# A hybrid decoder step on one core: another hand-over order for the mixer's streams

## The chip, the cores and the metric

The kernel runs on one core of a Trainium2 chip. The core's engines work side by side and meet at semaphores: TensorE (PE, with its weight loads shown as PEld), VectorE (DVE), ScalarE (ACT), GpSimd (POOL) and SyncE (SP). SP computes nothing and starts nearly all loads; POOL starts the gathered ones. The metric is the device time of one execution in microseconds (us).

## The reference

One step of a decoder layer for a prompt of 256 tokens and 64 sample tokens (8 sequences of 8), width 1024, all in float32:

```python
h = x * (1.0 + scale) + shift                     # from adaln(c): silu(c) @ w_ada + b_ada
rq, rk, rv, rg, mq, mk, mv = project(h, w_in, pos)  # one projection, split by columns
o_ret, ret_state = retention_fn(rq, rk, rv, log_g)  # 4 heads with decay
o_moba = moba_fn(mq, mk, mv)                        # 4 heads, top-3 blocks of cached K/V + own block
mixed = concat([group_norm(o_ret) * silu(rg), o_moba]) @ w_o
x = layer_norm(ALPHA * x + gate * mixed, ln_g, ln_b)
x = layer_norm(ALPHA * x + gate_f * (relu(h_f @ w_up) ** 2 @ w_down), ...)
```

The sample tokens attend to 1024 cached positions each, found through a page table; keys and values of the cache are gathered page by page. The new keys, values and retention states are outputs too.

## The kernel before

The kernel has three stretches on PE: a first one that prepares the modulation (adaLN), the modulated input `hT` and the projection `zq` (0 to 63.5 us in the trace); the mixer (63.5 to 286.9 us); and the feed-forward part (FFN) with its weights `up` and `dn` (to the end). The change concerns the mixer alone.

Nearly all the mixer's data are weights and cache pages that are used once. They come in tiles of 512 KB through one ring of ten slots (tag "wr", `WR = 10`, line 135). A load can start only when the slot's last reader is done: an ACT and a DVE instruction for projection weights, which are split into a high and a low part (`split1`, lines 177 and 179), a DVE transpose for cached keys (line 612), a matmul for adaLN weights (line 567) and cached values (line 703). SP starts its loads strictly in its own order (line 189, and line 320 for pages of V), and so does POOL (line 602 for keys, line 303 for every other page of the second half of V): an early load whose slot isn't free holds back all behind it.

The mixer's work is written as about forty generators, "streams", each of which issues a few instructions per step. The names that the text uses:

- `qk`, `mv`, `rv`, `rg`: the projections (lines 439 to 445), `lqk` ... `lrg`: their weight loads and splits
- `ga`, `gs`, `gc`: three adaLN products, eight tiles each (`Ada.step`, line 567); the sum with the bias, `gao`, `gso`, `gco`, is a DVE instruction (line 572)
- `G0`, `G1`: gathers of cached keys `kp` for two groups of four sequences; `K0`, `K1`: the transposes into the one tile `kt` (line 612), the scores `psS` (line 619) and the softmax, whose probabilities are turned by `pp` (line 677)
- `V0`, `V1`: pages of V and their products `po` (line 693 for the new tokens, line 703 for the cache); `h0` to `h3`: prompt heads; `rs`, `r0`, `r1`, `st`: the prompt's retention
- `sr`: the sample's retention: `pos` (lines 861, 864), its group norm `gs_r`, `gs_n`, `gs_y` (lines 766 to 778, on DVE, POOL and ACT), its transpose `pt7` (line 873) and the new state `pns` (line 884), for which POOL builds `vx` (line 881)
- `wl`, `w00` ... `w23`: the out-projection's weights `wo` and its products `pw`; `xl`: three loads of `x` into slots that earlier held the turned queries and keys `qkT` and the values `mvA`; `n0` to `n2`: the layer norm; `ul`, `u0`, `us`: the first FFN block

What sets the order of the mixer's work is one text, `SCHEDULE` (line 98). Each word names a stream, `*n` repeats it, and the loop at line 1188 takes one step of that stream:

```python
for step in SCHEDULE.split():
    name, _, n = step.partition("*")
    for _ in range(int(n or 1)):
        next(run[name])
```

The framework beneath keeps each engine's instructions roughly in this order, hands out slots in it, and places waits by data. So the text decides the order on all five engines at once, and with the slots also what each load has to wait for.

Of the kernel before, what the change touches and what calls it, by code (L numbers as in the profile page):

```python
# [25 lines left out]
T = SEQ + NB * TS  # L26
# [69 lines left out]


SCHEDULE = """
lqk*2 qk lmv qk*2 lmv qk mv ga G0 ga T mv ga G0 ga T ga*2 mv*2 ga T qk T*2 gs lmv*2 gs mv T mv
gs mv G0 mv ga K0 tb ga mv K0 G0 K0 mv qk mv G0 gs lqk*2 qk G0 gs K0 mv qk*3 gs K0 lrv K0 lrv  # L100
rv gs ov G0 rv gs rv gs qk*2 ok rv*2 lrv rv lrv ro K0 ro rT rv rT G0 rv ov ro rT ok gc rv K0*2
rv*2 G0*3 gc K0*2 rv lrg*2 K0*2 rg G0 rg G0 K0 gc*2 K0 G0 rg K0*2 rg G0 rg G0 K0*2 gc G1 rg K1
K0 lrg K0 G1 lrg K0 G1 rg rs G1 K1*3 gc G1 rg G1 rg*2 K1 gc*2 V0*4 rg*2 sw G1 K1 h0 sw rs gc r0
mx sw K1 sw sr h1 h0 K1 G1 h3 V0 r1 G1 V0 K1 G1 h0 h1 G1 r0 V0 G1 K1 sw*2 V0 G1 K1 G1 sr h2 K1
G1 V0 K1 V0 K1 h2 r1 G1 K1 sr K1 sr wl K1 h3 K1 st K1*2 wl w10 wl K1 h1 xl sr w00 K1 V1 w00 h2
w10 h3 w11 w20 w21 w11 wl V0 w01 w21 w20 w02 ul V1 gt w02 st w01 w03*2 w12 sc V1 w12 V1 w13 xl
n0 w13 n0 V1 ul n0 n1 n0 n1 V1*5 xl V1 n0 n1*2 u0 w23 w22 ul*2 w23 n1 u0 w22 n2*4 us u0*5 us u0
us
"""


# [1264 lines left out]
```

## Time and profile before

| | |
|---|---|
| median of 3 runs | 522.01 us (520.49 to 522.8) |
| the profiled execution | 523.97 us, span of its instructions 522.2 us |
| mean granted TensorE clock | 0.984 of full speed |
| busy PE, PEld, DVE, ACT, POOL | 490.8, 371.0, 320.2, 191.5, 119.4 us |
| moved by DMA | 122.80 MB, mean 235 GB/s |

A share of the span is an average: PE is busy for 94% of it, and the other 6% lie at a few places that the views by window and by wait show. "Granted clock" is the share of full speed (2.4 GHz) that PE got; at 0.5 it runs at its lower level, 1.2 GHz, and each matmul takes about twice as long, without any idle time being shown.

### The profile page before, as it was taken

To read this page: it belongs to the slowest core of one execution; us is meant where nothing else is said; L and a number is where in the kernel's file an instruction comes from. 1 tells how busy PE (TensorE), PEld (TensorE's weight loads), DVE (VectorE), ACT (ScalarE), POOL (GpSimd) and SP (SyncE) were. 2 spreads that over 40 slices of the span, in tenths; PEclk is the share of its full clock that TensorE was granted. 3 is DMA by queue.
4 is the path that set the end of the run, shared out by engine and by line. 5 is a ranking of instruction groups with operands and counts; after the bars stand their busy time and mean duration, and the time that the engine had idled before them with its cause. 6 is when DMAs were issued, how large, how long until landed. Compare 5 with 4: busy or idle time off the path is not lost.

```text
span 522.2 us, 8092 instructions
## 1 busy us (share of the span) xinstructions
PE 490.8 (94%) x3012; PEld 371.0 (71%) x3012; DVE 320.2 (61%) x549; ACT 191.5 (37%) x336; POOL 119.4 (23%) x125
## 2 busy tenths in 40 slices
PE   6899997999979999999898999999999999999993
PEld 4656864667645554576377977979898898989783
DVE  2444885359866777975584698533526263556776
ACT  1332712323125334370356532524325252545300
POOL 5000033424612454166320095000000000000030
PEclk9999999999979999999999999999999999999997
DMA  8999889999999988798952946626464381510011
GB/s 210 337 396 372 284 274 341 320 349 351 329 405 293 314 306 313 260 374 309 320 200 67 385 153 216 236 93 225 159 242 162 128 277 66 199 40 0 1 37 64
DMA packets 55313, 122.80 MB, mean 235 GB/s; under 512 B 5129, under 2 KB 17841, under 8 KB 55274
## 3 DMA queue, kind: packets, MB, share of 16 engines
q1 hardware_dynamic: 47690, 98.86, 54.2%
q0 software_dynamic: 7040, 22.76, 12.3%
q10 hardware_dynamic: 544, 0.67, 0.4%
q8 instruction: 23, 0.38, 0.3%
q14 instruction: 16, 0.13, 0.1%
HBM read 118.40 MB, written 3.87 MB: 234 GB/s over the span
## 4 chain that ended last, share of the span: by engine, by line
PE 79%; DMA 9%; DVE 6%; issue 1%; ACT 1%; POOL 1%; SPq 1%; DVEq 0%; POOLq 0%; ACTq 0%
PE pu L1120 7%; PE pu L1119 7%; PE pu L1121 7%; PE acc L443 5%; PE acc L444 5%; PE acc L445 5%; DMA wa<-in_w_ada_dram 4%; PE po L703 3%; PE acc L440 3%; PE psS L619 3%; PE acc L439 3%; DMA gc<-in_w_ada_dram 2%; DMA kp<-in_cache_k_dram,idx 2%; PE pw L443 2%; PE pw L445 1%
## 5 line engine op out<-in xcount | busy, mean ns | idle before, releaser
L602 POOL DMA_INDIRECT kp<-in_cache_k_dram,idx x32 | 35.1, 1098 | 80.1 <-DMA mv<-in_w_in_dram 41.9
L612 DVE STREAM_TRANSPOSE kt<-kp 128x1024 f32<-128x1024 f32 x32 | 38.3, 1225 | 8.5 <-PE psS L619 4.8
L1053 POOL TENSOR_TENSOR l22r<-l22r,mhalf 64x1 f32<-64x1 f32 x1 | 1.0, 987 | 176.0 <-DVE l22r L1051 176.0
L1227 DVE TENSOR_TENSOR usq<-relu 128x320 f32<-128x320 f32 x32 | 16.6, 524 | 36.3 <-ACT relu L1222 36.2
L1222 ACT ACTIVATE relu<-pu 128x320 f32<-128x320 f32 x28 | 12.1, 431 | 46.7 <-PE pu L1121 46.7
L703 PE MATMUL po<-v,PT 128*32 128x512 f32 x128 | 25.5, 601 | 1.6 <-DMA v<-in_cache_v_dram,idx 1.6
L199 ACT ACTIVATE uT<-usq 128x320 fp32r<-128x320 f32 x32 | 15.0, 467 | 21.8 <-DVE usq L1227 21.8
L303 POOL DMA_INDIRECT v<-in_cache_v_dram,idx x16 | 18.6, 1164 | 9.4 <-DMA v<-in_cache_v_dram 4.1
L202 DVE TENSOR_TENSOR uT<-usq,uT 128x256 fp32r<-128x256 f32 x32 | 15.7, 490 | 6.9 <-ACT uT L199 6.5
L619 PE MATMUL psS<-kt,qd 128*32 128x256 f32 x256 | 18.1, 382 | 0.2 <-DVE kt L612 0.2
L383 PE MATMUL pm<-wa,cT 128*32 128x256 f32 (+1 forms) x160 | 12.1, 384 | 3.5 <-DMA wa<-in_w_ada_dram 3.5
L1204 POOL TENSOR_TENSOR x<-x,lng 128x512 f32<-128x512 f32 (+1 forms) x6 | 9.0, 1523 | 23.9 <-DMA lng<-in_ln_g_dram 23.9
L619 PEld LDWEIGHTS psS<-kt,qd 128*32 128x32 f32 x256 | 8.7, 110 | 7.4 <-issue 2.4
L391 DVE COPY mn<-pm 128x256 f32<-128x256 f32 (+1 forms) x5 | 1.9, 370 | 18.8 <-PE pm L383 18.8
L1205 POOL TENSOR_TENSOR x<-x,lnb 128x512 f32<-128x512 f32 (+1 forms) x6 | 12.8, 2155 | 0.0
L383 PEld LDWEIGHTS pm<-wa,cT 128*32 128x32 f32 x160 | 5.8, 128 | 9.1 <-DMA wa<-in_w_ada_dram 4.7
L703 PEld LDWEIGHTS po<-v,PT 128*32 128x32 f32 x128 | 4.5, 109 | 10.6 <-issue 5.9
L567 PE MATMUL gsp<-gs,cT 128*32 128x256 f32 x64 | 6.6, 482 | 3.2 <-DVE gao L572 3.2
L203 DVE TENSOR_TENSOR uT<-usq,uT 128x64 fp32r<-128x64 f32 x32 | 9.2, 286 | 0.0
L567 PE MATMUL gcp<-gc,cT 128*32 128x256 f32 x64 | 5.8, 420 | 2.9 <-DMA gc<-in_w_ada_dram 2.9
L881 POOL TENSOR_TENSOR vx<-rv,tabt 64x1024 f32<-64x1024 f32 x4 | 7.5, 1889 | 3.6 <-PE pos L861 1.9
L1042 DVE SCALAR_TENSOR_TENSOR x<-x,zlo 128x512 f32<-128x512 f32 (+1 forms) x12 | 8.1, 684 | 0.3
(1359 smaller groups left out, 1599.9 us busy)
## 6 DMA issues: line engine op xcount, KB each, us to landing
dn<-in_w_down_dram SPq DMA_DIRECT2D x32, 512.0 KB
v<-in_cache_v_dram SPq DMA_DIRECT2D x48, 256.0 KB
wa<-in_w_ada_dram SPq DMA_DIRECT2D x16, 512.0 KB
wi<-in_w_in_dram SPq DMA_DIRECT2D x8, 512.0 KB
ga<-in_w_ada_dram SPq DMA_DIRECT2D x8, 512.0 KB
gs<-in_w_ada_dram SPq DMA_DIRECT2D x8, 512.0 KB
gc<-in_w_ada_dram SPq DMA_DIRECT2D x8, 512.0 KB
wo<-in_w_o_dram SPq DMA_DIRECT2D x8, 512.0 KB
```

Of the source, the lines that this page charges most:

```text
L303: nc.gpsimd.indirect_dma_start(out=dst, out_offset=None, in_=table, in_offset=bass.IndirectOffsetOnAxis(ap=idx[:, b * NPG + s:b * NPG + s ...
L383: pm_last.append(nc.tensor.matmul(pm[32 * j:32 * j + 32, 0:128 * nf], cT[:, k, :], wa[c, s_, k // per][:, k % per, :], start=(k < 2), stop ...
L443: nc.tensor.matmul(acc, hi, wh, start=first, stop=False)
L444: nc.tensor.matmul(acc, lo, wh, start=False, stop=False)
L445: nc.tensor.matmul(acc, hi, wl, start=False, stop=last)
L602: nc.gpsimd.indirect_dma_start(out=kp.rearrange("p c f -> p (c f)"), out_offset=None, in_=ck_pairs, in_offset=bass.IndirectOffsetOnAxis(ap ...
L612: nc.vector.transpose(kt[:, 2 * i:2 * i + 2].rearrange("p c f -> p (c f)"), kps[g, n, i].rearrange("p c f -> p (c f)"))
L619: nc.tensor.matmul(psS[n // 2][32 * h:32 * h + 32, cols].rearrange("p (c l e) -> p c e l", l=32, e=2), qd[:, g, 4 * h + j, :], kt[:, :, 12 ...
L703: nc.tensor.matmul(po[32 * b:32 * b + 32, :], PT[:, b, s, :], vt[b // 2][:, b % 2], start=False, stop=(s == NPG - 1), skip_group_check=True)
L1119: nc.tensor.matmul(pu[:, toks], wh, hi, start=first and k == ks[0], stop=False)
L1120: nc.tensor.matmul(pu[:, toks], wl, hi, start=False, stop=False)
L1121: nc.tensor.matmul(pu[:, toks], wh, lo, start=False, stop=last and k == ks[-1])
```

## The change

Only the text `SCHEDULE` is another one; every stream's code, all tiles and all buffers are the same. Its start, as an example of the whole:

```diff
 SCHEDULE = """
-lqk*2 qk lmv qk*2 lmv qk mv ga G0 ga T mv ga G0 ga T ga*2 mv*2 ga T qk T*2 gs lmv*2 gs mv T mv
+T lqk lmv lqk lmv ga mv*2 ga T mv G0 qk*2 ga mv qk G0 mv T ga*3 qk G0 lmv K0 tb gs lmv T K0 lqk
...
```

What it does is seen in the engines' own orders. Three places follow; in the rows a name's digits after the underscore are a buffer's number.

On PE, at the change from the first adaLN product to the second (`gap` and `gsp` are their sums, `ga7` and `gs0` the last and the first weight tile), before:

```order
L567 MATMUL gap_706<-ga7_879,cT_81 32x256 x4
L443 MATMUL qkz1_661<-qk01h_655,hT_199 128x512
L444 MATMUL qkz1_661<-qk01h_655,hT_199 128x512
L445 MATMUL qkz1_661<-qk01l_656,hT_199 128x512
L567 MATMUL gsp_820<-gs0_821,cT_81 32x256 x4
L567 MATMUL gsp_820<-gs1_839,cT_81 32x256 x4
```

and now:

```order
L567 MATMUL gsp_817<-gs0_818,cT_81 32x256 x4
L567 MATMUL gap_692<-ga6_845,cT_81 32x256 x4
L443 MATMUL qkz1_732<-qk00h_667,hT_199 128x512
L444 MATMUL qkz1_732<-qk00h_667,hT_199 128x512
L445 MATMUL qkz1_732<-qk00l_668,hT_199 128x512
```

The first piece of `gsp` has moved ahead of the last two pieces of `gap`; `ga7` follows 21 rows later. On DVE `gao`, the instruction that reads the finished `gap`, stands behind the transposes of `kp002` and `kp003` in both orders; before, `gsp` took the bank that `gap` gives back, and now the two are open at the same time in different banks.

On PE, around tile 5 of the third adaLN product (`gcp`; `kt03` is the last quarter of the first group's keys), before:

```order
L619 MATMUL psS01_888<-kt03_1296,qd_643 32x4x2x32 x16
L439 MATMUL rgz2_1244<-rg10h_1355,hT_199 128x512
L440 MATMUL rgz2_1244<-rg10l_1356,hT_199 128x512
L439 MATMUL rgz2_1244<-rg10h_1355,hT_199 128x512
L440 MATMUL rgz2_1244<-rg10l_1356,hT_199 128x512
L567 MATMUL gcp_1162<-gc5_1447,cT_81 32x256 x4
L439 MATMUL rgz2_1244<-rg11h_1405,hT_199 128x512
```

and now:

```order
L439 MATMUL rgz2_1185<-rg10h_1362,hT_199 128x512
L440 MATMUL rgz2_1185<-rg10l_1363,hT_199 128x512
L439 MATMUL rgz2_1185<-rg10h_1362,hT_199 128x512
L440 MATMUL rgz2_1185<-rg10l_1363,hT_199 128x512
L631 MATMUL pn_1383<-mkT_174,mqT_173 32x64 x4
L567 MATMUL gcp_1102<-gc5_1427,cT_81 32x256 x4
L567 MATMUL gcp_1102<-gc6_1433,cT_81 32x256 x4
L439 MATMUL rgz2_1185<-rg11h_1375,hT_199 128x512
L440 MATMUL rgz2_1185<-rg11l_1376,hT_199 128x512
```

`gc5` stood 31 rows behind the scores of `kt02` (row 476) and now stands 38 behind them (475 to 513); `gc6`, which stood 17 rows after `gc5`, follows it at once. On SP the loads of `gc5`, `gc6` and `gc7` follow each other in both orders; the slots that they take are now those of `kp031`, `kp032` and `kp033`, before they were those of `kp031`, `gc4` and `kp100`. The tiles `kp102` and `kp103` took their slots ahead of `gc5` and now do so behind `gc7`. Two adaLN products were cut in two by other work (`gs3`, `gc7`), and now three are (`ga1`, `gs1`, `gc4`).

On PE, near the end of the first group's values (`po0`; `v060` to `v072` are page tiles, `pos` is the sample's retention), before:

```order
L703 MATMUL po0_1503<-v060_2017,PT_1402 32x512
L861 MATMUL pos_2069<-st0_1738,qb0_1752 128x128 x2
L703 MATMUL po0_1503<-v060_2017,PT_1402 32x512
L861 MATMUL pos_2069<-st0_1738,qb0_1752 128x128 x2
L864 MATMUL pos_2069<-rv2_636,As_1742 128x128 x2
L861 MATMUL pos_2069<-st1_1740,qb1_1756 128x128
L703 MATMUL po0_1503<-v062_2038,PT_1402 32x512
L861 MATMUL pos_2069<-st1_1740,qb1_1756 128x128 x6
L703 MATMUL po0_1503<-v062_2038,PT_1402 32x512
L861 MATMUL pos_2069<-st1_1740,qb1_1756 128x128
L864 MATMUL pos_2069<-rv2_636,As_1742 128x128 x2
```

and now:

```order
L703 MATMUL po0_1512<-v060_2080,PT_1426 32x512
L861 MATMUL pos_2041<-st0_1737,qb0_1751 128x128 x8
L864 MATMUL pos_2041<-rv2_636,As_1741 128x128 x2
L861 MATMUL pos_2041<-st1_1739,qb1_1755 128x128 x8
L864 MATMUL pos_2041<-rv2_636,As_1741 128x128 x2
L703 MATMUL po0_1512<-v060_2080,PT_1426 32x512
L703 MATMUL po0_1512<-v062_2101,PT_1426 32x512 x2
L703 MATMUL po0_1512<-v070_2129,PT_1426 32x512 x2
L703 MATMUL po0_1512<-v072_2150,PT_1426 32x512
L619 MATMUL psS11_1324<-kt12_2031,qd_643 32x4x2x32 x9
L703 MATMUL po0_1512<-v072_2150,PT_1426 32x512
L619 MATMUL psS11_1324<-kt12_2031,qd_643 32x4x2x32 x7
```

The rows of `po0` stood one by one between other products and now mostly stand next to each other. The same holds from `v030` on.

Two more moves are told in words. On POOL `gs_r` stood between `vx0` and `vx1`, behind the gather of `kp133`; now it stands behind `vx1` and behind the first gather for the second group's values, `v100`. On SP the third load of `x` (`x2`, into the slot of `mvA`, whose last reader is the product of line 693 for the second group) stood behind all pages of V, as the last load of the mixer; now it stands ahead of `up03`, `wo30`, `wo31` and the pages `v120` to `v172`.

## Rows read from the trace of the kernel before

**Rows 1.** The windows view: busy us by engine, granted clock, DMA share, GB/s.
```profile
60.00:260.00 200.00, 188.97 (x1233) 115.38 (x1231) 139.40 (x243) 69.93 (x150) 79.92 (x82) 0.97 0.91 323
63.47:286.90 223.43, 209.23 (x1378) 133.11 (x1377) 154.55 (x275) 83.57 (x174) 83.39 (x85) 0.98 0.84 301
```

**Rows 2.** The view of waits of PE: total us, times, longest.
```profile
PE gsp L567 <- DVE gao L572: 3.2, 1, 3.2
PE gcp L567 <- DMA gc<-in_w_ada_dram: 2.9, 1, 2.9
PE pt L873 <- DVE gs_y L778: 1.7, 1, 1.7
PE po L703 <- DMA v<-in_cache_v_dram,idx: 1.6, 1, 1.6
```

**Rows 3.** The windows view again, in stretches of 4 us.
```profile
88.00:92.00 4.00, 2.96 (x25) 1.24 (x26) 2.11 (x3) 0.00 (x0) 2.72 (x6) 0.62 0.73 231
...
152.00:156.00 4.00, 3.82 (x15) 2.44 (x16) 4.00 (x7) 0.60 (x1) 0.00 (x0) 0.50 1.03 393
156.00:160.00 4.00, 4.00 (x23) 2.52 (x21) 2.19 (x6) 0.91 (x2) 0.94 (x1) 0.85 0.90 271
...
256.00:260.00 4.00, 2.00 (x6) 0.18 (x4) 0.61 (x3) 0.40 (x2) 0.56 (x1) 1.00 0.94 311
```

**Rows 4.** The chain that ended last, 84 to 92 us: start, us, what.
```profile
79.87 8.69 DMA kp<-in_cache_k_dram,idx
...
88.60 0.40 DVE gao L572
...
89.04 2.79 PE gsp L567 x24
```

**Rows 5.** The same chain, 128 to 156 us.
```profile
129.84 0.23 PE rvz L445
130.07 0.57 PE gcp L567 x8
130.64 1.77 PE psS L619 x32
...
140.17 2.38 DVE kt L612 x2
...
142.62 9.52 DMA gc<-in_w_ada_dram
```

**Rows 6.** The timeline of PE, 174 to 198 us: start, us, operation, count.
```profile
177.97 1.06 PE L703 MATMUL po<-v,PT 128*32 128x512 f32 x8
178.97 0.49 PE L727 MATMUL pS<-mkT,mqT 128*128 128x128 f32 x2
...
183.22 1.04 PE L703 MATMUL po<-v,PT 128*32 128x512 f32 x2
184.19 0.49 PE L753 MATMUL pop<-STp,mvA 128*128 128x128 f32 x2
```

**Rows 7.** The chain, 196 to 200 us, and the timeline of PE at 209 us.
```profile
197.92 0.64 PE pos L864 x4
...
209.46 0.41 PE L873 MATMUL pt<-ident,gs_y 128*128 128x128 f32 x2 [1.68 <-DVE gs_y L778]
```

**Rows 8.** The page's costliest groups: busy us, mean ns | idle before, releaser.
```profile
L612 DVE STREAM_TRANSPOSE kt<-kp 128x1024 f32<-128x1024 f32 x32 | 38.3, 1225 | 8.5 <-PE psS L619 4.8
...
L303 POOL DMA_INDIRECT v<-in_cache_v_dram,idx x16 | 18.6, 1164 | 9.4 <-DMA v<-in_cache_v_dram 4.1
...
L881 POOL TENSOR_TENSOR vx<-rv,tabt 64x1024 f32<-64x1024 f32 x4 | 7.5, 1889 | 3.6 <-PE pos L861 1.9
```

**Rows 9.** The chain, 252 to 260 us.
```profile
252.34 6.14 DMA v<-in_cache_v_dram,idx
...
258.52 1.06 PE po L703 x2
```

More of the change, by code (lines that the diff above doesn't have):

```diff
@@ L98 @@
 SCHEDULE = """
-lqk*2 qk lmv qk*2 lmv qk mv ga G0 ga T mv ga G0 ga T ga*2 mv*2 ga T qk T*2 gs lmv*2 gs mv T mv
[L100 to L108, printed above, removed]
+T lqk lmv lqk lmv ga mv*2 ga T mv G0 qk*2 ga mv qk G0 mv T ga*3 qk G0 lmv K0 tb gs lmv T K0 lqk
+ok ga K0 mv*2 G0*2 mv lrv ga T qk lrv qk mv*2 K0 lqk rv gs*4 mv G0 gs K0 mv qk T ov gs qk K0 gs
+G0 qk K0 qk*2 K0 G0 qk G0*2 rv K0 rv ro rv gs gc lrv rT K0 ro G0 ov lrg rv lrv K0 lrg rT rv G0
+rg ga gc ro K0 rv rg G0 rv*2 rg K0 rv G0 ok K0*3 G0 rg K0 rv rT G0 gc rv gc rg G1 gc K1 mx K0
+rs K0*2 lrg G1 K1 rg lrg rg K0 gc*2 rg gc G1*2 gc K1*2 G1 K0 rg K1 rg*2 V0*2 rg G1 K1 G1 h0 K1
+sw V0 sw G1 rs sw V0 r0 sr h1 V0 sw h3 r1 V0 h0 K1 h0 K1 r0 G1*2 xl V0 K1 G1 sw h1 G1 h2 K1*2
+xl sw G1 sr V0 K1 G1 V0 G1 K1*2 r1 G1 h2 K1 st V0 h1 h2 h3 K1*5 wl sr w00 K1 sr V1 xl sr V1 wl
+w10 h3 st w20 w10 w11*2 w00 gt w21 wl sc V0 w21 w01 w12 w20 w02 V1 w12 ul w02 wl w01 ul w03*2
+V1 n0 V1 w13 n0*2 ul n0 w13 n0 V1 n1*2 V1*4 n1 V1 n1*2 ul w23 u0 w22 w23 w22 n2*3 u0 n2 us u0*4
+us u0*2 us
 """
```

## The prediction

> **What bounds the kernel now.** I read the windows first. In the mixer, from 63.47 to 286.90 us, PE is busy for 209.2 of 223.4 us at a mean clock of 0.98, while DVE, ACT and POOL lie far below [rows 1]. So PE sets the pace, and the mixer can shorten only where PE idles, runs at the lower clock, or does its own work more slowly than it can. The first qkz matmul and the first pu matmul bound this stretch; what lies outside keeps its order, so I cost it at nothing. The windows also show the limit next to PE: between 60 and 260 us the DMA engines are busy for 0.91 of the time at 323 GB/s, about 18 us of 200 idle [rows 1].
>
> The waits of PE come next. Four matter: 3.2 us of gsp for gao, 2.9 of gcp for its weights, 1.7 of pt for gs_y, 1.6 of po for the last pages of V [rows 2]. The short windows show what the two long ones cost beyond themselves: the granted clock is 0.62 in 88 to 92, and 0.50 and 0.85 in 152 to 160; behind the 1.6 us wait it stays at 1.00 [rows 3]. A clock of c over a window of 4 us loses 4 × (1 − c): 1.5 us after the first, 2.0 + 0.6 = 2.6 after the second.
>
> The chain names the causes. Gao starts at 88.60, after keys that took 8.69 us to land and the DVE work on them; gsp starts 0.04 behind its end [rows 4]. The gc wait: two transposes of kt from 140.17 free a slot, and the load that takes it lands 9.52 us after 142.62 [rows 5].
>
> The last view is PE's timeline of po. Eight po matmuls side by side take 177.97 to 178.97, 1.00 us; two alone take 183.22 to 184.19, 0.97 us [rows 6]. Cutting po into pairs thus costs 0.97 − 0.25 = 0.72 us per isolated pair, without any idle time.
>
> **The change part by part.**
>
> *gs0.* The first gsp piece no longer takes the bank that gao empties, and ga6, ga7 and projection work follow it. That wait goes with its clock loss: 3.2 + 1.5 = 4.7 us gained. Gao and the key transposes are as late as before, but no PE instruction near them asks for them.
>
> *gc5.* Between the scores of kt02 and gc5 there are now 30 matmuls of 0.235, a score block of 1.77, three and a half adaLN pieces of 0.57 and two small products, 11.7 us of PE work; before it was 24 + 4 matmuls, one score block and one piece, 8.9 us (durations of [rows 5]). The two transposes that free the slot and the load take 2.4 + 9.5 = 11.9 us. So gc5 itself fits nearly; gc6 and gc7, one and two transposes later, follow at once, and I leave 1.3 us of wait, too short for the clock to fall if it goes by the 1.6 us case. Gain 2.9 + 2.6 − 1.3 = 4.2. The ends: nothing gained, or 5.5.
>
> *po.* In the trace of before seven pairs stand alone as at 183.22 (one each of v030, v042 and v072, two each of v060 and v062); now one does, the first of v060: 6 × 0.72 = 4.3 gained, PE not being idle there. In the second group v150 is cut by a transpose of x: at most 0.7 lost, taken whole. Net 3.6.
>
> *Cut adaLN pieces.* Three instead of two; a piece of eight takes 0.57, and I charge one more of that, 0.6 lost.
>
> *Softmax of the second group.* Its transposed probabilities (pp) now come 8.8 us of PE work after the scores of kt03, before 10.0, and on DVE they stand behind transposes of kp102 and kp103, whose gathers now compete with gc5 to gc7. Before, PE waited nothing here. Lower end 0; upper end the 1.2 us less, and 1.5 MB at 323 GB/s more ahead, 4.6 us: 5.8. I take 2.5, nearer to the row without a wait.
>
> *v070 and v072.* Their slots come from kp120 and kp121, which can be transposed only once kt11's scores are read. Landing as in [rows 9], 6.14 us, plus one or two transposes of 1.2 [rows 8], against 8.2 to 9.9 us of PE work: between 0 and 2.5 us of wait. I take 1.5.
>
> *gs_y.* Before, the last pos product ended at 198.56 and pt7 began at 209.46, 10.9 us with 1.7 of wait [rows 7]. Now PE has about 7.8 us of work between them (four and a half po rows, a score block, small products, three pw). With an equally long chain the wait is 3.1; DVE has lost a state update from it. Between 0 and 3.1 I take 2.2: 0.5 lost.
>
> *Early loads* (mv11, ga7): ga7 stands behind 0.64 MB of outputs, 2.0 us at 323 GB/s; between 0 and 2.0, I take 0.7.
>
> *End of V.* x2 now blocks SP until the second group's first po; behind it lie 7.75 MB: x2, three weight tiles and twelve tiles of V. At 323 GB/s they take 24 us, beside about 25 us of PE work up to v172 (its rows by the durations above), but the last tile also needs its landing. Before, the wait was 1.6; I take 2.5, 0.9 lost, with 0 and 4.8 as ends.
>
> Everything else (projections, heads, norms, out-projection) is the same work in another place and I cost it at nothing: on PE it only changes neighbours, on ACT and DVE there is slack.
>
> Sum: −4.7 − 4.2 − 3.6 + 0.6 + 2.5 + 1.5 + 0.5 + 0.7 + 0.9 = −5.8 us. The profiled execution's span of 522.2 becomes 516.4 and its time, 523.97 with 1.8 us around the span, 518.2. That execution lies 2.0 above the median of the runs shown, so the median should go from 522.0 to 516.2.
>
> **Rivals.**
>
> *The gc wait is one of bandwidth and stays.* In 152 to 156 us the DMA engines are at 1.03 [rows 3]; the gathers of kp102 and kp103 and three gc tiles ask for them together. If gc5 lands as late as before relative to PE, 4.2 of the gain go, and the time is 520.4. For it: the full DMA share. Against it: about 18 us of idle DMA time around, and 2.8 us more PE work ahead of gc5. The Trainium skill (Trainium Kernel Development and Optimization, Key Constraints) says that loads issued from SP, ACT and POOL run on the same 16 DMA engines and interleave, so that a further issuer saves only issue time: by that, another order brings nothing faster where the share is full, which speaks for this rival. The trace agrees as far as it goes, with 1.03 while SP and POOL both had loads under way.
>
> *x2 holds the pages back.* At 323 GB/s and 6.14 us of landing the last tile comes 30 us after x2 is let go, against 25: a wait of 4.8, and with it a clock loss as at 152 us, 2.6. That is 4.9 more than I charged: 521.1.
>
> *The sample's readout chain becomes the stop (slower).* Gs_r on POOL waits for vx1, 1.9 us, and for a gather, 1.2, that itself needs a free slot; gs_y on DVE stands behind two kt13 transposes, 2.5 [rows 8], whose keys may land late by a landing of 6.1 [rows 9]. All of it makes the chain 10.9 + 11.7 = 22.6 us, beside 7.8 of PE work: a wait of 14.8 and 2.6 of clock, 15.2 more than I charged: 531.4. It decides for slower as soon as wait and clock exceed 2.2 + 5.8 + 2.6 = 10.6 us, a chain of about 16 us; at 13.6, 2.7 more than before, the sum is about even. For it: four queues meet there. Against it: POOL and DVE have reached these rows early in the trace of before.
>
> *The new waits don't come.* The four costs for pp, v070, gs_y and early loads, and the end of V, sum to 6.1; without them 510.
>
> **How the numbers follow.** Forecast 0.55, no new waits 0.12, gc wait stays 0.15, x2 0.10, readout chain 0.08. A measurement of this kernel tells about 0.5%, 2.6 us, from no change. The forecast's own terms leave about 3 us either way, so 0.47 of its 0.55 are faster, the rest the same; of the gc and x2 rivals a sixth is faster and a little slower. Faster 0.63, same 0.25, slower 0.12. The range starts below the case without new waits, at 508, and ends at 525, halfway into the readout chain.
>
> **What would show it.** Right: no wait of gsp for gao and a clock of 1.00 around PE's first gsp; gcp waits under 2 us and no window below 0.9 after it; one isolated po pair between v030 and v072. Pp, po of v070 and pt7 should show waits of 1 to 3 us. Wrong: a gc wait near 3 us with the clock at 0.50 behind it, or a wait of 5 us or more before pt7 or the last po, or mixer waits at places that I name nowhere; a first pu matmul at 286 us or later would refute the sum.

## The result and the profile after

The changed kernel takes 513.86 us (median of four runs, 513.0 to 515.26) against 521.25 for the kernel before, run beside it (520.47 to 522.8): a ratio of 0.9857 [0.9821, 0.9894], 7.4 us less. The forecast was 516.2. The profiled executions differ by more, 523.97 against 513.0, because the one of before lies 2.7 above the median of its runs here and the one of after 0.9 below.

Three marks divide the profiled span: the first matmul behind the first stretch (of `qkz` before, of `gap` after), the first `po0` matmul, and the first `pu` matmul on the tile `up10`.

| | before | after |
|---|---|---|
| first matmul of the mixer | 63.47 | 63.27 |
| first `po0` matmul | 168.03 | 157.89 |
| first `pu` matmul on `up10` | 286.90 | 276.23 |
| front of the mixer (63 to `po0`) | 104.6 | 94.6 |
| back of the mixer (`po0` to `pu`) | 118.9 | 118.3 |
| FFN (from `pu` on) | 235.3 | 234.9 |

So the front is 10 us shorter, the back 0.6. The windows view of the kernel before, from 80 us to its first `po0` (columns as in [rows 1]: window, its length, busy us of PE, PEld, DVE, ACT, POOL, granted clock, DMA share, GB/s):

```profile
80.00:168.03 88.03, 81.32 (x558) 52.33 (x556) 56.73 (x84) 25.78 (x48) 30.38 (x34) 0.94 0.96 340
```

The same view of the kernel after: first the whole mixer (from 0.1 us ahead of its first matmul), then its front to the first `po0`, then stretches of the front.

```profile
63.17:276.23 213.06, 204.37 (x1378) 133.48 (x1378) 157.12 (x277) 83.99 (x174) 84.43 (x85) 0.98 0.87 317
80.00:157.89 77.89, 76.69 (x564) 50.09 (x562) 56.13 (x85) 25.40 (x46) 32.81 (x38) 1.00 1.00 371
88.00:92.00 4.00, 4.00 (x27) 2.91 (x20) 1.36 (x2) 1.61 (x2) 0.00 (x0) 1.00 0.96 359
140.00:160.00 20.00, 19.55 (x175) 11.34 (x174) 16.65 (x36) 6.54 (x21) 7.72 (x10) 1.00 1.02 396
```

Nearly the same 560 matmuls of the front now take 76.69 us instead of 81.32, since the clock is 1.00 and not 0.94, and PE idles 77.89 − 76.69 = 1.2 us instead of 6.7. The DMA engines, which were at 0.96, are at 1.00. The stretches that answer to [rows 3] show no lower clock: 1.00 in 88 to 92 and 1.00 in 140 to 160, at a DMA share of 1.02.

The waits of PE in the mixer answer to [rows 2] (total us, times, longest; rows of the other stretches left out):

```profile
PE px L1088 <- DVE mixT L208: 2.0, 1, 2.0
PE pw L445 <- DVE wo01l L179: 1.6, 1, 1.6
PE px L1088 <- DVE l11r L1051: 0.9, 1, 0.9
...
PE pw L445 <- DVE wo00l L179: 0.8, 1, 0.8
```

All four waits of [rows 2] are gone: none of gsp, gcp or `pt7`, and the page puts 0.2 us on `po`. In their place stand waits that the prediction names nowhere, two at the first out-projection products (`pw`, for the low part of `wo00` and `wo01`) and two in the layer norm (`px`). The windows show what they cost beyond themselves:

```profile
200.00:204.00 4.00, 2.36 (x10) 1.24 (x10) 4.00 (x5) 1.06 (x1) 3.21 (x2) 1.00 0.76 304
204.00:208.00 4.00, 4.00 (x11) 0.93 (x7) 2.98 (x8) 0.00 (x0) 0.97 (x1) 0.55 0.58 174
208.00:212.00 4.00, 4.00 (x11) 3.19 (x12) 2.41 (x6) 1.58 (x7) 1.92 (x2) 0.60 0.78 229
252.00:256.00 4.00, 4.00 (x17) 3.46 (x16) 2.94 (x7) 2.44 (x7) 0.00 (x0) 0.57 0.97 391
```

Reckoned as in the prediction, 4 × (1 − c), the clock costs 1.8 + 1.6 = 3.4 us after the two `wo` waits and 1.7 in the layer norm. DVE is busy for 4.00 of 4 us ahead of them, and the DMA share falls to 0.58. Three timelines tell why (start, us, operation, count, and in brackets the idle time before and what ended it). DVE:

```profile
196.88 2.73 DVE L179 TENSOR_TENSOR wo00l<-wo,wo00h 128x1024 fp32r<-128x1024 f32 x1
199.53 0.21 DVE L653 TENSOR_REDUCE bmx<-sn 128x1 f32<-128x64 f32 x1
199.66 2.79 DVE L179 TENSOR_TENSOR wo01l<-wo,wo01h 128x1024 fp32r<-128x1024 f32 x1
```

POOL:

```profile
196.63 4.73 POOL L881 TENSOR_TENSOR vx<-rv,tabt 64x1024 f32<-64x1024 f32 x2 [3.54 <-PE pns L884]
201.52 1.85 POOL L303 DMA_INDIRECT v<-in_cache_v_dram,idx  x1 [0.16 <-issue]
```

PE:

```profile
199.67 0.73 PE L445 MATMUL pw<-wo00l,mixT 128*128 128x512 f32 x2 [0.83 <-DVE wo00l L179]
...
202.50 0.51 PE L445 MATMUL pw<-wo01l,mixT 128*128 128x512 f32 x1 [1.64 <-DVE wo01l L179]
```

The two splits of `wo` take 2.73 and 2.79 us on DVE while POOL builds two `vx`. In the trace of before the same splits took 1.21 each, none of the four `vx` fell beside them, and this pair of `vx` took 3.75:

```profile
205.28 3.75 POOL L881 TENSOR_TENSOR vx<-rv,tabt 64x1024 f32<-64x1024 f32 x2 [1.70 <-PE pns L884]
209.23 1.21 DVE L179 TENSOR_TENSOR wo00l<-wo,wo00h 128x1024 fp32r<-128x1024 f32 x1
211.30 1.21 DVE L179 TENSOR_TENSOR wo01l<-wo,wo01h 128x1024 fp32r<-128x1024 f32 x1
```

The falling DMA share is SP's doing. Its timeline and the row of its waits:

```profile
196.33 0.32 SPq L189 DMA_DIRECT2D gb<-in_ln_b_dram  x1
207.99 1.17 SPq L189 DMA_DIRECT2D gA<-gscr  x2
210.61 2.41 SPq L320 DMA_DIRECT2D v<-in_cache_v_dram  x2
```

```profile
SPq L189 <- PE pns L884: 11.3, 1, 11.3
```

The step `gt` loads the two tables of the gates (`gA`, line 1028) into a ring of four buffers in which `vx` and the retention's states lie too, and SP's wait shows whose reader it needs: `pns`, the product of `vx`. From 196.65 to 207.99 SP stands before `gA`, and pages of V and tiles of `up` wait behind it.

Of the work on PE that was to shrink, the page's group of `po` fell from 25.5 to 21.1 us:

```profile
L703 PE MATMUL po<-v,PT 128*32 128x512 f32 x128 | 21.1, 601 | 0.2 <-DMA v<-in_cache_v_dram 0.2
```

Where that saving went shows in the windows view of the whole back, before and after:

```profile
168.03:286.90 118.87, 111.38 (x705) 69.52 (x705) 82.84 (x177) 54.18 (x119) 47.03 (x45) 1.00 0.76 275
157.89:276.23 118.34, 110.85 (x710) 72.50 (x710) 85.15 (x178) 54.20 (x119) 45.60 (x41) 0.96 0.78 280
```

PE idles for the same 7.49 us in both, and the clock is 0.96 where it was 1.00. The new waits have taken the place of those that went, and the slower clock behind them (3.4 + 1.7 = 5.1 us as reckoned above) uses up about what PE saved.

### The profile page after: what moved, and what is told of

The parts are those of the page before. It is cut to its first block, busy times and chain, and to the rows that moved or that the text cites. A ratio compares the mean times of both kernels' runs of the same rounds, so it can differ in the third digit from the quotient of the medians.

```text
span 511.1 us, 8076 instructions
## 1 busy us (share of the span) xinstructions
PE 486.1 (95%) x3012; PEld 370.9 (73%) x3012; DVE 321.3 (63%) x549; ACT 191.7 (37%) x336; POOL 119.7 (23%) x125
## 2 busy tenths in 40 slices
DMA packets 55312, 122.80 MB, mean 240 GB/s; under 512 B 5129, under 2 KB 17841, under 8 KB 55274
## 4 chain that ended last, share of the span: by engine, by line
PE 83%; DVE 7%; DMA 5%; ACT 2%; issue 1%; SPq 1%; DVEq 0%; POOL 0%; ACTq 0%
PE pu L1119 7%; PE pu L1120 7%; PE pu L1121 6%; PE acc L445 6%; PE acc L443 6%; PE acc L444 5%; DMA wa<-in_w_ada_dram 4%; PE acc L440 3%; PE acc L439 3%; PE po L703 3%; PE psS L619 3%; PE pw L443 2%; PE pw L445 2%; PE pw L444 1%; PE zq L443 1%; PE zq L445 1%
## 5 line engine op out<-in xcount | busy, mean ns | idle before, releaser
L1227 DVE TENSOR_TENSOR usq<-relu 128x320 f32<-128x320 f32 x32 | 17.7, 559 | 36.9 <-ACT relu L1222 36.6
L703 PE MATMUL po<-v,PT 128*32 128x512 f32 x128 | 21.1, 601 | 0.2 <-DMA v<-in_cache_v_dram 0.2
L303 POOL DMA_INDIRECT v<-in_cache_v_dram,idx x16 | 18.5, 1159 | 11.1 <-PE po L703 4.3
L1204 POOL TENSOR_TENSOR x<-x,lng 128x512 f32<-128x512 f32 (+1 forms) x6 | 10.2, 1739 | 22.9 <-DMA lng<-in_ln_g_dram 22.9
L1205 POOL TENSOR_TENSOR x<-x,lnb 128x512 f32<-128x512 f32 (+1 forms) x6 | 10.8, 1823 | 0.0
L881 POOL TENSOR_TENSOR vx<-rv,tabt 64x1024 f32<-64x1024 f32 x4 | 8.6, 2156 | 6.9 <-PE pns L884 3.5
L409 ACT ACTIVATE hT<-xT,mT 128x256 fp32r<-128x256 f32 x8 | 4.5, 594 | 10.0 <-DVE mT L395 9.9
L1105 DVE TENSOR_SCALAR h2f<-px,scT,shT 128x128 f32<-128x128 f32 x16 | 6.3, 408 | 3.0 <-ACT h2T L1104 2.9
```

The lines of the kernel that those rows point to most:

```text
L303: nc.gpsimd.indirect_dma_start(out=dst, out_offset=None, in_=table, in_offset=bass.IndirectOffsetOnAxis(ap=idx[:, b * NPG + s:b * NPG + s ...
L703: nc.tensor.matmul(po[32 * b:32 * b + 32, :], PT[:, b, s, :], vt[b // 2][:, b % 2], start=False, stop=(s == NPG - 1), skip_group_check=True)
L1227: nc.vector.tensor_mul(u, r, r)
```

## The experiments

All ratios are to the kernel before, run beside the variant on the same chip, with a 95% interval. Every edit but one changes only the words of `SCHEDULE`. A splice takes one text up to a named step and the other from there on, each with the steps that are then still due; every stream keeps its own number of steps.

**Which half gains.** Two splices at the first `V0`:

```diff
front_only:  new order up to the first V0, then the old one
back_only:   old order up to the first V0, then the new one
```

> Up to the first step of V0 the new order, from there the remaining steps in the old order. Theory A (the whole gain is made before the first po0, by the two adaLN waits and the clock behind them, and nothing takes it back): first po0 near 158 us, and from there about 119 us as in the old order, so 511 to 513 us, no slower than the new order's 513.9. Theory B (loads are the limit, so a front that is 10 us earlier only waits longer for pages of V or weights later): po or pw waits for loads of 3 us and more, 516 to 520 us. Theory C (the uncut po pieces carry half of the gain, as the sum had it with 3.6 of 5.8): about 517 us.

Measured: 517.05 against 523.51, 0.9891 [0.9856, 0.9927], 6.5 us less, against 7.4 for the whole new order. That misses theory A and is the time of B and C; but no load keeps PE waiting for more than 0.6 us in the mixer (against B), and the next run speaks against C. The first `po0` matmul comes at 158.9, and its front reads like that of after:

```profile
80.00:158.90 78.90, 76.82 (x562) 49.86 (x560) 55.22 (x84) 25.04 (x46) 34.15 (x38) 1.00 0.98 357
```

> Up to the first step of V0 the old order, from there the remaining steps in the new order. Theory A: both old adaLN waits stay with their clock, first po0 near 168 us, the rest as long as in the new order (118 us): 520 to 522 us, no different from the kernel before. Theory C: po pieces and the waits for gs_y and the last pages of V gone: 514 to 518 us.

Measured: 523.50 against 523.51, 0.9994 [0.9962, 1.0026]. The new order of the back half, with the cheaper `po`, brings nothing by itself that can be measured. Its profiled execution is the shortest of its twelve (517.87, 5.6 below their median), and it shows something on the clock. The wait of gsp is there (2.0 us; 3.2 in before), yet the clock stays up in 88 to 92:

```profile
88.00:92.00 4.00, 4.00 (x32) 2.28 (x24) 1.24 (x2) 1.03 (x2) 3.79 (x8) 1.00 0.90 287
```

In before it was 0.62 there [rows 3], behind the longer wait; in gc_only below it is 0.57 behind a wait of 2.0 us too. What follows the same wait thus isn't the same in every execution.

**Whether the front's two terms add.** Two more splices part them:

```diff
gs_front:  new order up to the last gs piece (gs7), then the old one
gc_only:   old order up to gs7, the new one to the first V0, then the old one
```

> The new order up to the last weight tile of the second adaLN product (gs7), from there the old one: gsp no longer waits for gao, and gc5 to gc7 have their old places and slots. Theory A (the two waits are worth about 5 us each and add up): the gsp wait is gone, the gcp wait of 2.6 to 2.9 us stays with its clock, first po0 near 163 us, 4 to 6 us below the kernel before. Theory B (loads are the limit): PE comes earlier to gc5, but the load does not, and the gcp wait grows by the 5 us that were won: within 1.5 us of the kernel before. Theory G (the slower clock after gsp falls in some runs only, so that piece is worth 2 to 3 us): 2 to 3 us below.

Measured: 520.53 against 521.97, 0.9986 [0.9963, 1.0008]. No wait of gsp, and the first `po0` comes at 164.8, 3.2 before that of the old order; but the other wait is still there, and one of `po` has grown to 2.0 us:

```profile
PE gcp L567 <- DMA gc<-in_w_ada_dram: 2.7, 1, 2.7
PE po L703 <- DMA v<-in_cache_v_dram,idx: 2.0, 1, 2.0
```

By the first `pu` matmul on `up10`, at 286.88, the lead is lost: behind the wait of `po` the clock is 0.58 and 0.57 in 256 to 264, 3.4 us by the same reckoning, where it stayed at 1.00 behind the 1.6 us of before. But this execution (524.16) is the slowest of its nine, 3.6 above their median; by the medians gs_front is 1.4 us below the kernel before, which can't be told from nothing.

> The old order up to gs7, then the new one up to the first step of V0, then the old one: gsp waits for gao as before, gc5 to gc7 have their new places and slots, V0 and all behind it are the old order. Theory A (the two pieces are worth about 5 us each by themselves): no gcp wait, 4 to 6 us below the kernel before. Theory J (gs_front alone brought 0.7 us because the lead was lost again at gc5 and at the last pages of V, so the gc piece carries nearly all of what front_only gained, 5.7 us): 5 to 6 us below. Theory K (the two pieces are worth something only together, since either wait delays the loads of the other): 1 to 3 us below.

Measured: 523.15 against 523.30, 1.001 [0.9976, 1.0045]. Now the wait of gcp is gone and that of gsp is there, with a new one of `pp`, the transposed probabilities of the first group (the product `po0` follows at 165.71):

```profile
PE pp L677 <- DVE P L668: 2.1, 1, 2.1
PE gsp L567 <- DVE gao L572: 2.0, 1, 2.0
```

And the clock falls at both places, in 88 to 92 and behind `pp`:

```profile
88.00:92.00 4.00, 4.00 (x29) 2.20 (x24) 0.93 (x1) 0.00 (x0) 3.90 (x8) 0.57 0.90 285
...
160.00:180.00 20.00, 17.06 (x98) 7.44 (x97) 12.78 (x37) 6.39 (x18) 4.88 (x5) 0.83 0.80 286
```

Either piece alone is worth nothing that can be measured, at most 0.4% by the intervals; both together, in front_only, are worth 1.1%. This is the case that the expectation of gc_only calls K, though not even its 1 to 3 us are seen; and gs_front has the time of its theory B, but the wait of gcp did not grow. The splices show that the two are worth more together than apart. The traces show, in one execution each, which waits and which slower stretches take the place of the one removed; why these come there was not followed further.

**The waits at `wo`.** Either POOL's `vx` holds DVE's splits up, or the splits simply come too late in the order. One run takes half of POOL's work away, the other moves the splits:

```diff
 vx_half (lines 877 to 881; the last two vx are not built, the first two are read again):
-            pn = [bank("pns") for _ in range(2)]
+            pn, vxs = [bank("pns") for _ in range(2)], vxs if pr else []
...
-                vx = r4(f"vx{h}", [64, 8, 128])
-                nc.gpsimd.tensor_tensor(vx, rvN[2][:, None, 128 * h:128 * h + 128].to_broadcast([64, 8, 128]),
+                vx = vxs[hp] if pr else r4(f"vx{h}", [64, 8, 128])
+                pr or vxs.append(vx) or nc.gpsimd.tensor_tensor(vx, rvN[2][:, None, 128 * h:128 * h + 128].to_broadcast([64, 8, 128]),
 wo_split_early:
-K1 st V0 h1 h2 h3 K1*5 wl sr w00
+K1 st V0 h1 h2 h3 wl K1*5 sr w00
```

> The new order, with POOL building only vx0 and vx1; the second pair of state products reads these two again (a part of the computation is left out: two POOL products of 1.9 to 2.4 us, and the second pair's state is not the reference's). Theory D: nothing runs on POOL beside the splits of wo00 and wo01, which take 1.2 us each in the same place of DVE's order; PE's waits for them fall from 2.5 us to under 0.5 and the clock stays at 1.00. Rival F (the splits are slow for another reason, such as their place or the loads that land at that time): still 2.7 us each.

Measured, a single run: 513.16. DVE's timeline:

```profile
197.99 1.21 DVE L179 TENSOR_TENSOR wo00l<-wo,wo00h 128x1024 fp32r<-128x1024 f32 x1
199.11 0.21 DVE L653 TENSOR_REDUCE bmx<-sn 128x1 f32<-128x64 f32 x1
199.24 1.22 DVE L179 TENSOR_TENSOR wo01l<-wo,wo01h 128x1024 fp32r<-128x1024 f32 x1
```

Without POOL beside them the same splits, at the same place in the order, take 1.21 and 1.22 again; the waits of `pw` are gone, and the clock is 1.00 from 200 to 212. So it is POOL, and not the place. Yet the span is 511.3, no shorter than that of after (511.1): PE waits and the clock falls further on instead (next run).

> The new order, with the first out-projection weight load and split (wl) five steps earlier, ahead of the last key transposes. Theory D (DVE's two splits of wo00 and wo01 take 2.7 us instead of 1.2 because POOL builds vx2 and vx3 at the same time, and PE's two waits for them, 2.5 us, bring 7 us at half clock, 3.4 us lost): the splits run before vx2, at 1.2 us each, both waits go and the clock stays at 1.00 around 205 us: 508 to 510 us. Rival E (the stretch is limited by the loads of wo10 and x behind it, or by kt13, and the wait moves to the next instruction): kt13's scores wait 2 us longer, 513 to 515 us.

Measured: 514.75 against 523.51, 0.9826 [0.9788, 0.9863], which can't be told from the new order's 0.9857. The splits take 1.23 and 1.18 at 193.57 and 196.99, and PE no longer waits for them. What stops PE instead, 20 us later, shows in the chain that ended last (start, us, what):

```profile
211.91 8.70 DMA up<-in_w_up_dram
...
220.72 1.06 ACT up02h L177
...
221.81 1.23 DVE up02l L179
223.03 0.10 DVE gbT L1011
223.17 0.90 PE pt L715 x3
```

PE waits 2.5 us for `gbT`, a small DVE copy of the layer norm's scales (line 1011) that stands on DVE behind the split of an `up` tile; that tile's load was issued late by SP, at 211.9, behind `gA` and two pages of V. In vx_half the same wait has 2.2 us, and the clock behind it is 0.57 in 220 to 224.

**SP's gate loads.** The step `gt`, which holds SP, is moved behind the last `w03`, alone and together with the earlier split:

```diff
 gates_only:
-w00 gt w21 wl sc V0 ... ul w03*2 V1 n0
+w00 w21 wl sc V0 ... ul w03*2 gt V1 n0
 gates_late: the same, and
-K1 st V0 h1 h2 h3 K1*5 wl sr w00
+K1 st V0 h1 h2 h3 wl K1*5 sr w00
```

> The new order with the gate loads (gt) moved as in gates_late and wl where the new order has it. Theory O (each of the two edits is hidden behind the other's wait, as wo_split_early by itself gave little): PE still waits about 2.5 us for wo00l and wo01l with 7 us at half clock behind it, and the time is within 1.5 us of the new order, 512.5 to 515 us. Rival P (the gate loads alone are what held the back half): 509 to 511 us, as gates_late.

Measured: 515.20 against 523.83, 0.9835 [0.9795, 0.9876], not to be told from the new order's. SP runs on, but the waits for `wo00l` and `wo01l` (0.8 and 1.6 us) are still there, and so is the clock behind them:

```profile
204.00:208.00 4.00, 4.00 (x10) 1.47 (x9) 3.03 (x7) 0.00 (x0) 2.40 (x3) 0.50 1.00 355
```

> The new order with wl five steps earlier as in wo_split_early, and besides the gate loads (gt) moved from behind w00 to ahead of the fourth step of V1. Theory H (in wo_split_early SP stands about 11 us at the gate loads, whose slots the pns products still read; up02, wo30 and the pages of V behind them come late, and DVE waits in its queue for up02, with gbT and pt behind it: so the wait moved there): SP issues v110 and up00 to up03 from 198 us on instead of 208, the pt wait behind gbT goes, 507 to 510 us. Rival I (the slots of the ring, not the gate loads, hold these loads back): SP waits at v110 or up00 as long, and the time stays at 513 to 515 us.

Measured: 509.67 against 521.97, 0.9776 [0.9757, 0.9795]. The windows and SP's timeline:

```profile
204.00:208.00 4.00, 3.28 (x15) 2.31 (x14) 3.29 (x12) 0.60 (x3) 2.19 (x3) 1.00 1.06 409
208.00:212.00 4.00, 4.00 (x23) 3.03 (x22) 2.08 (x7) 3.89 (x12) 0.12 (x1) 1.00 1.03 401
```

```profile
196.67 0.35 SPq L189 DMA_DIRECT2D gb<-in_ln_b_dram  x1
198.21 1.59 SPq L320 DMA_DIRECT2D v<-in_cache_v_dram  x2
200.66 4.12 SPq L189 DMA_DIRECT2D up<-in_w_up_dram  x4
```

The 11.3 us of SP are gone, the DMA share is 1.03 to 1.06 where it was 0.58 to 0.78, and 23 matmuls fall into 208 to 212 where 11 did. Neither edit alone changes the time by more than the intervals allow; the two together take 4.4 us off the new order (509.67 against 514.09 of new_again, run beside it). The traces show the case that the expectation of gates_only calls O: with either edit alone PE still waits, at `wo` or for `gbT`, with the slower clock behind it, and with both it does not. By the times alone a plain sum isn't excluded: the edits took 0.3% and 0.2% off by themselves, each with an interval of about 0.4% either way, and 0.8% together. This kernel is faster than the kernel before and the new order, and none found here is measurably faster.

> The new order once more, unchanged, to stand beside the other runs of this set on the same chip: 0.982 to 0.990 of the kernel before.

Measured: 514.09 against 521.97, 0.9855 [0.9838, 0.9872]: the changed kernel once more, to compare the next run and gates_late with. The first `po0` comes at 158.2, PE's waits are those of after.

**The rival of x2.** The third `xl`, which loads `x2`, is moved behind all pages of V:

```diff
-K1 sr V1 xl sr V1 wl ... V1*4 n1 V1 n1*2
+K1 sr V1 sr V1 wl ... V1*4 n1 V1 xl n1*2
```

> The new order with the third load of x (x2) behind all pages of V, as in the order before. The rival in which x2 holds back the pages and costs 4.9 us would make it 3 to 5 us faster than the new order; if x2 held nothing back that PE waits for (po waited 0.2 us in the new order's trace), no difference beyond 1.5 us.

Measured: 516.42 against 521.97, 0.9893 [0.9874, 0.9912]: not faster than the new order but 2.3 us slower than new_again. So `x2` did not hold the pages back. The waits at `wo` are still there, and the clock is 0.50 from 204 to 212 and 0.84 in 240 to 260. By the same reckoning the clock costs 8.4 us in the mixer of this profile and 5.1 in that of new_again, which would cover the 2.3; why it falls further is not settled.

**What `po` in one piece is worth.** The second `sr` step goes two `V0` steps later, so that its `pos` products cut `po` up again:

```diff
-G1 sr V0 K1 G1 V0 G1 K1*2
+G1 V0 K1 G1 V0 sr G1 K1*2
```

> The new order with one step moved: the second step of sr (the pos products) two V0 steps later, ahead of a G1 step, so that four more po rows (v060 to v072) stand alone among the pos products; nothing else is moved but their neighbours. By the price of the sum, 0.72 us for an isolated pair, PE's own work grows by 2.9 us. Theory A (the back half is PE's): 2.5 to 3.5 us slower than the new order, 516.5 to 517.5 us. Theory L (the back half is held by the loads that SP issues behind the gate loads, so that PE's own work there is hidden): PE waits 2 to 3 us less at wo00l and wo01l, and the time is within 1.5 us of the new order.

Measured: 516.41 against 523.30, 0.9885 [0.9835, 0.9934]. The page's group:

```profile
L703 PE MATMUL po<-v,PT 128*32 128x512 f32 x128 | 24.5, 602 | 0.6 <-DMA v<-in_cache_v_dram 0.6
```

PE does 24.5 − 21.1 = 3.4 us more for the same matmuls, and of that 0.9885 − 0.9857, about 1.5 us, reaches the time, with intervals that overlap. The edit also took the wait for `wo00l` away, so it is no clean measure. How much of the 3.4 counts is not shown: neither all of it nor none is excluded, and so neither of the two theories.

**The layer norm.** In gates_late the last `V1` goes ahead of the third `n1`:

```diff
-V1*4 n1 V1 n1*2
+V1*5 n1*3
```

> As gates_late, with the last step of V1 (pt5, the transpose of the second group's output) ahead of the third step of n1 instead of behind it. Theory M (in gates_late pt5 waits 2.3 us because its bank is the one that h2f still reads for the layer norm, and with the waits around it the clock falls for 7 us, about 2.7 us): pt5 waits for o_s alone, 1 us, and the clock stays at 1.00 from 244 to 256 us: 505 to 507.5 us, 2 to 4 us below gates_late. Rival N (the layer norm's chain over DVE, ACT and POOL is what ends last here, so the wait moves to px): 509 to 511 us.

Measured: 510.10 against 523.30, 0.9761 [0.9713, 0.9809], no different from gates_late. The wait that it was to remove is still there, so the run says nothing on what that wait is worth:

```profile
PE pt L715 <- DVE h2f L1105: 2.3, 1, 2.3
```

## Why the prediction was right, and where it was not

The direction was right, and the size near: 5.8 us less forecast, 7.4 measured, at 513.86 inside the range. The steps fared less evenly.

*gs0 (4.7).* Right in what it removes: no wait of gsp, and a clock of 1.00 in 88 to 92. *gc5 (4.2).* Under-sized: the 1.3 us of wait left in it didn't come, and the gain is the 2.9 + 2.6 = 5.5 that the text gave as its upper end. Together these are 10.2, and the profiled fronts differ by 9.9: 5.5 of idle time (6.7 to 1.2) and 4.4 of PE's busy time, where the prediction reckoned 4.1 for the clock. What the sum does not show is that the two belong together: alone they gave 0.9986 and 1.001, with the wait of the other still there and others behind it (`po` 2.0, `pp` 2.1); only together they gave 0.9891.

And as a term of the median, the 10 us of the front are too much: front_only gave 6.5. Its profiled front is 8.3 us shorter than that of before (96.3), but that execution is one of its faster ones, 1.8 below the median, while the profiled one of before is only 0.5 above the median of the runs beside front_only. Where the other executions of front_only lose time is open. That the clock differs from one execution to the next is shown: behind 2.0 us of wait of gsp it was 1.00 in back_only and 0.57 in gc_only, and in the kernel before the mean clock was 0.972 in a run of 527.08 us and 0.996 in one of 519.49.

*po (3.6).* The mechanism was right and its size on PE as well: 4.3 forecast before the one cut, 25.5 − 21.1 = 4.4 measured. But the back of the mixer fell by 0.6 us only, and back_only measured 0.9994. The saving is not lost on an idle PE: it idles for 7.49 us of the back before and after. By this reckoning it went into the slower clock behind the new waits (5.1), so what failed here is the zero for those places, below.

*The new waits (6.1 in all: pp 2.5, v070 and v072 1.5, gs_y 0.5, early loads 0.7, end of V 0.9).* Over-sized: PE waited for none of them for longer than 0.2 us. For v070 and v072 the terms written there give 0.3 at most (6.14 + 2.4 − 8.2), not the 2.5 of the text. The sample's readout ended in time; `pt7` begins at 194.00 without a wait:

```profile
194.00 0.38 PE L873 MATMUL pt<-ident,gs_y 128*128 128x128 f32 x2
```

Pp, which the prediction puts into the second group's softmax though it is the first group's, did wait 2.1 us in gc_only, close to the 2.5, but there the lead that the first piece gives was missing. The cut adaLN pieces (0.6) were not measured apart.

*"Everything else ... I cost it at nothing ... on ACT and DVE there is slack."* This is the step that failed. The two waits at `wo` (0.8 + 1.6) with their clock (3.4), and the layer norm's waits (2.0 + 0.9 and 0.7 for `h2f`) with theirs (1.7), are 11.1 us at places that the prediction doesn't name, and its own list of what would prove it wrong has such waits on it. That the size came out near is in part luck. The terms of the front (gs0, gc5, cut pieces, pp, early loads) sum to 5.1 us gained, and the profiled front gained 9.9; those of the back (`po`, v070, gs_y, end of V) sum to 0.7, and it gained 0.6, because the waits that were priced and did not come, and the old ones that went, stand against those that nobody priced. The profiled spans differ by 11.1 us, the medians by 7.4.

The rivals: that the gc wait is one of bandwidth is refuted, since it went entirely while the DMA share was 1.02. The order decided which loads came first, and that was enough: both kernels move 122.80 MB. The sentence cited from the Trainium skill beside it (Trainium Kernel Development and Optimization, Key Constraints) is on which queue issues a load; that another order brings nothing where the share is full was the prediction's own step from it, and it did not hold here. X2 is refuted by x2_late. The readout chain did not become the stop. The case in which no new wait comes, 510, was right on the waits it lists and wrong on the time, for the places above.

## What to carry to other kernels

Terms of one stretch in which the waits hang on one ring of buffers and one queue of loads need not add: splice the old and the new order at a few steps, and see which pieces pay alone. Work saved on the busiest engine can be lost again in the same stretch, to new waits and a slower clock behind them; price the hand-overs (an engine that works in order, a load that blocks its queue) before crediting it. When a removed wait changes nothing, look for the second one that it was hiding, and remove both. Compare a profile with the median of its kernel before reading a size off it.

## What the runs showed of the hardware

A DVE tensor-tensor of 128x1024 with two inputs took 1.21 us alone and 2.73 to 2.79 beside POOL's tensor-tensor. POOL's pair took 4.73 us instead of 3.75. Take POOL's work away, and DVE's is at 1.21 again, so POOL's work is the cause (vx_half). One after another the four instructions would take 2 × 1.21 + 3.75 = 6.2 us; side by side they took 5.8 (196.63 to 202.45), so hardly anything was gained, as if one engine stood still while the other finished. The Trainium skill (SBUF — State Buffer, SBUF: two separate sides) says that a DVE operation with two inputs in SBUF and a GpSimd operation that reads SBUF take one shared pair of ports as an exclusive lock for a whole instruction, and that the loser blocks. The durations here agree with that; no run shows the ports themselves.

TensorE's granted clock was 0.55 and 0.60 in 204 to 212, about half of full speed, behind two waits of 0.83 and 1.64 us with a few matmuls between them, whereas after the single 1.6 us wait of before it stayed at 1.00 [rows 3]. And behind the wait of gsp, 2.0 us in back_only and in gc_only, it was 1.00 in the one execution and 0.57 in the other.
